# Moving the loads of the attention tables and small weights behind those of the bias tables in an encoder layer on one Trainium2 core

## The chip, the cores and the metric

The kernel runs on one NeuronCore of one Trainium2 chip. The metric is device time in microseconds (us) of one execution; lower is better. The profile is one execution recorded by the hardware profiler. TensorE does the matmuls (PE in the rows, PEld for its weight loads), VectorE is DVE, ScalarE is ACT, GpSimd is POOL, and SyncE (SP, its queue SPq) issues every load and store of this kernel.

## The reference

One layer of a hybrid encoder over 768 tokens (512 of one request, 256 of another) of width 1024. One input projection feeds three groups of heads: A is chunked spatial gating, B differential attention with a distance penalty, C neighbourhood attention on a 64-wide grid with a learned bias. Cut to what matters here:

```python
h = x @ w_in                                   # 768 x 1024 -> u, v (A); q, k, v (B); q, k, v (C)
out_a = gelu(u) * (w_s @ layer_norm(gelu(v), a_ln_g, a_ln_b) + b_s)
lam = exp(sum(lq1 * lk1)) - exp(sum(lq2 * lk2)) + lam_init
out_b = rms_norm((softmax(q1 k1 - slope * dist) - lam * softmax(q2 k2 - slope * dist)) v, subln_g) * (1 - lam_init)
out_c = softmax(q k + bias(rpb)) v             # over a window of rows and 16 columns
x = layer_norm(alpha * x + concat(out_a, out_b, out_c) @ w_out)
x = layer_norm(alpha * x + (silu(x @ w_gate) * (x @ w_up)) @ w_down)
```

## The kernel before, in words

All matmuls run at full fp32 accuracy by splitting: each operand becomes a high part in fp32r (a ScalarE cast, line 113) and a low part (source minus high part, line 114, mostly on VectorE), and three matmuls stand for one product. An operand is thus ready only when a load has landed, ScalarE has cast it and VectorE has subtracted.

**The opening** (lines 262 to 295) computes q and k of branch C. The contraction over 1024 is done in eight steps k of 128. Step k needs tile k of the transposed input, 384 KB (`load_x`, line 230), and every second step a weight tile of 512 KB (`w_load`, line 121). In each step TensorE does 24 matmuls into eight PSUM regions (`cqk_mm`, line 258): for each of four column groups f, first high input with high weights, then low input (`xlo`), then high input with low weights. Inputs and weights share three buffers of the pool `raw`, so a load goes out when the split of an earlier tile has freed one. In what follows w1 is the second weight tile (steps 2 and 3), and x2 and x3 are the inputs of steps 2 and 3.

**After the loop**, in the text of the kernel, come the loads of small tables (lines 298 to 312): `dist` (448 KB, branch B's distances), `lq` (four vectors of 64), `subg` (128 values), `alng` and `alnb` (256 values each), `wsT` (256 KB) and `bsT` (2 KB). The seven vectors are read through `broadcast_rows`, which sends one row of memory to all 128 partitions. Lines 314 to 323 then make `neglam` (two VectorE reductions at 318, a ScalarE Exp at 320, two small VectorE operations) and scale `subg` (line 323).

**Behind them** stand the evacuation of C's q and k from PSUM (`c_evac`, lines 335 to 355), the load of `mask` (line 378, 128 x 1408 fp32, which is 704 KB), and for each of four heads twelve small loads of the relative bias (`rpb`, lines 385 and 390) with seven GpSimd operations that make the bias tables `cb` (lines 394 and 400). Then come the projections of C's v, B, A, with the attention units of C (`c_unit`, line 489) from 7.75 on the kernel's own cost clock and those of B (`b_unit`, line 565) from 61.0 mixed between them, the output projection, and the feed-forward layer (lines 1010 and 1043), which is about two thirds of the time.

What sets the order: TensorE's order is the order of the program text (`manual_schedule`, line 79), with costs and due times written out by hand (lines 34 to 43). The order on every other engine and on SP's queue is set by the framework's scheduler, which simulates the program and gives each engine what is ready, earlier program text first. So a load whose buffer is free from the start may be issued long before the text around it. Within an engine or queue instructions start in the order so chosen; one that waits holds those behind it. In the rows the loads of lines 299 to 312 stand in SP's queue amid the loads of the opening.

`tc.issue_after(ins)` makes the instructions that its block issues on `ins`'s queue stand behind `ins` there, without a wait for its end.

Of the kernel before, what the change touches and what calls it, by code (L numbers as in the profile page):

```python
# [8 lines left out]
F32 = mybir.dt.float32  # L9
F32R = mybir.dt.float32r  # L10
ALU = mybir.AluOpType
AF = mybir.ActivationFunctionType
PSUM = bass.MemoryType.PSUM

P = 128
# [9 lines left out]
LAM0 = 0.8 - 0.6  # L25
# [28 lines left out]
def broadcast_rows(ap, n):  # L54
    return bass.AP(tensor=ap.tensor, offset=ap.offset, ap=[[0, P], [1, n]])
# [3 lines left out]
def encoder_layer(ctx: ExitStack, tc, a, o):  # L59
    nc = tc.nc  # L60
    V, S, G, TE = nc.vector, nc.scalar, nc.gpsimd, nc.tensor
# [179 lines left out]
    attp = att.enter_context(tc.tile_pool(name="att", bufs=1, reuse_waits="tile"))  # L241
# [53 lines left out]
    w_done(3)  # L295


    dist = attp.tile([P, 896], F32, name="dist")
    nc.sync.dma_start(out=dist, in_=a["dist"])
    lq = attp.tile([P, 4, 64], F32, name="lq")  # L300
    for i, n in enumerate(("lq1", "lk1", "lq2", "lk2")):
        nc.sync.dma_start(out=lq[:, i], in_=broadcast_rows(a[n], 64))
    subg = attp.tile([P, P], F32, name="subg")
    nc.sync.dma_start(out=subg, in_=broadcast_rows(a["subg"], P))
    alng = attp.tile([P, 256], F32, name="alng")
    nc.sync.dma_start(out=alng, in_=broadcast_rows(a["alng"], 256))
    alnb = attp.tile([P, 256], F32, name="alnb")
    nc.sync.dma_start(out=alnb, in_=broadcast_rows(a["alnb"], 256))
    wsT = attp.tile([P, 4, P], F32, name="wsT")
    nc.sync.dma_start(out=wsT, in_=a["wsT"])  # L310
    bsT = attp.tile([P, 4], F32, name="bsT")
    nc.sync.dma_start(out=bsT, in_=a["bsT"])

    neglam = attp.tile([P, 1], F32, name="neglam")
    lsum = attp.tile([P, 2], F32, name="lsum")
    lpr = attp.tile([P, 64], F32, name="lpr")
    for i in range(2):
        V.tensor_tensor_reduce(out=lpr, in0=lq[:, 2 * i], in1=lq[:, 2 * i + 1], op0=ALU.mult, op1=ALU.add,
                               scale=1.0, scalar=0.0, accum_out=lsum[:, i:i + 1])
    S.activation(out=lsum, in_=lsum, func=AF.Exp)  # L320
    V.tensor_tensor(out=neglam, in0=lsum[:, 1:2], in1=lsum[:, 0:1], op=ALU.subtract)
    V.tensor_scalar(out=neglam, in0=neglam, scalar1=LAM0, scalar2=None, op0=ALU.subtract)
    V.tensor_scalar(out=subg, in0=subg, scalar1=1.0 - LAM0, scalar2=None, op0=ALU.mult)

    def qk_tiles():
# [51 lines left out]
    for h in range(4):  # L380
        t = mxp.tile([P, 1536], F32, tag="mx", name="cb")
        raw = mxp.tile([P, 1536], F32, tag="mx", name="rpb")
        src = a["rpbs"]
        for r in range(8):
            nc.sync.dma_start(out=raw[16 * r:16 * r + 16, 0:489],
                              in_=bass.AP(tensor=src.tensor, offset=src.offset + h * 945 + r * 63,
                                          ap=[[1, 16], [1, 489]]))
        src = a["rpbp"]
        for r in range(4):
            nc.sync.dma_start(out=raw[32 * r:32 * r + 32, 512:989],  # L390
                              in_=bass.AP(tensor=src.tensor, offset=src.offset + h * 1905 + (4 + r) * 127,
                                          ap=[[1, 32], [1, 477]]))
        for c0, n in ((0, 489), (512, 477)):
            G.tensor_scalar(out=raw[:, c0:c0 + n], in0=raw[:, c0:c0 + n], scalar1=8.0, scalar2=None, op0=ALU.mult)

        def fill(d0, nb, e, row, rows, cols):
            win = raw[:, e:e + 1]
            win = bass.AP(tensor=win.tensor, offset=win.offset, ap=[win.ap[0], [-cols, nb], [-row, rows], [-1, cols]])
            view = [x[:, d0:d0 + nb * P].rearrange("p (b r c) -> p b r c", b=nb, r=rows) for x in (t, mask)]
            G.tensor_tensor(out=view[0], in0=win, in1=view[1], op=ALU.subtract)  # L400


        fill(0, 2, 488 - 16, 63, 8, 16)
        fill(256, 3, 488, 63, 8, 16)
        fill(640, 2, 488, 63, 8, 16)
        for j in range(2):
            fill(896 + 256 * j, 2, 988 - 32 * (1 - j), 127, 4, 32)
        cbias.append(t)


    def proj_nat(w0, evac):
# [821 lines left out]
```

## Time and profile before

| | |
|---|---|
| runs | 893.86 us median of 3 (892.22 to 894.37) |
| the profiled execution's own time | 893.67 us |
| its span | 891.8 us |
| mean granted TensorE clock | 0.995 |
| TensorE busy | 846.5 us, 95% of the span |
| VectorE, ScalarE, GpSimd busy | 75%, 47%, 43% |
| DMA | 66.66 MB, 75 GB/s over the span |

The execution's time is 1.9 us over the span (start and end around the recorded instructions). Busy shares are averages over stages with different limits; what the change touches lies in the first 60 us. A row of a timeline reads: start, duration, engine, line, operation, output and inputs, shape, count, and in brackets the idle time before it with what ended it.

### The profile page before, as it was taken

How to read it: one execution, taken by the hardware profiler on the slowest of the kernel's cores; microseconds unless marked ns; L12 is line 12 of the kernel's file. 1: busy time of each engine (PE TensorE's matmuls, PEld its weight loads, DVE VectorE, ACT ScalarE, POOL GpSimd, SP SyncE). 2: the span in 40 equal slices, each digit the busy share in tenths (PEclk: the TensorE clock that was granted, in tenths of full speed). 3: DMA queues.
4: the chain of work that ended last, by engine and by line, in shares of the span. 5: the costliest groups of instructions: out<-in, count | busy, mean ns of one | idle time of the engine just before them, and what ended most of it. 6: DMA issues, size and time to landing. Idle time of an engine off the chain costs nothing. (4 is left out here: it accounts for less than half of the span.)

```text
span 891.8 us, 12955 instructions
## 1 busy us (share of the span) xinstructions
PE 846.5 (95%) x4811; PEld 754.3 (85%) x4811; DVE 666.9 (75%) x1168; ACT 422.0 (47%) x922; POOL 384.7 (43%) x320
## 2 busy tenths in 40 slices
PE   7999999999999998899999999999999999899996
PEld 6889897888987887898888898898888888789985
DVE  3574447576677568769989897988979797989577
ACT  3375477676665526544434444344444344344421
POOL 0580011100121148877655655555466464653235
PEclk9999999999999999999999999999999999999999
DMA  6830202011017101112212121222121222222222
GB/s 220 247 113 24 71 26 71 24 49 46 5 54 276 54 18 50 46 48 72 72 38 81 48 82 61 72 71 72 70 71 48 71 72 71 71 70 73 72 83 107
DMA packets 22160, 66.66 MB, mean 75 GB/s; under 512 B 3664, under 2 KB 5584, under 8 KB 22096
## 3 DMA queue, kind: packets, MB, share of 16 engines
q1 hardware_dynamic: 22096, 65.82, 22.4%
q8 instruction: 38, 0.62, 0.3%
q14 instruction: 26, 0.21, 0.1%
HBM read 62.67 MB, written 3.15 MB: 74 GB/s over the span
## 5 line engine op out<-in xcount | busy, mean ns | idle before, releaser
L114 DVE TENSOR_TENSOR w<-raw,w 128x512 fp32r<-128x512 f32 (+2 forms) x179 | 185.1, 1053 | 36.3 <-ACT w L113 35.4
L113 ACT CAST w<-raw 128x512 fp32r<-128x512 f32 (+2 forms) x213 | 138.3, 676 | 119.1 <-POOL raw L168 43.8
L1010 PE MATMUL ff<-x,w 128*128 128x384 f32 x600 | 109.9, 336 | 1.7 <-DVE bv L991 1.7
L1010 PEld LDWEIGHTS ff<-x,w 128*128 128x128 f32 x600 | 105.3, 188 | 3.5 <-DVE bv L991 2.0
L1010 PE MATMUL ff<-mix,w 128*128 128x384 f32 x480 | 91.8, 339 | 14.5 <-ACT snap L1021 6.5
L1010 PEld LDWEIGHTS ff<-mix,w 128*128 128x128 f32 x480 | 83.4, 188 | 19.3 <-DVE bv L1026 9.6
L444 PE MATMUL mm<-xhi,w 128*128 128x512 f32 x320 | 79.1, 346 | 0.4 <-DVE qs L341 0.4
L168 POOL TENSOR_TENSOR ws<-raw 128x512 f32<-128x512 f32 x29 | 41.2, 1424 | 79.2 <-DMA raw<-in_w 74.9
L168 POOL TENSOR_TENSOR raw<-raw 128x512 f32<-128x512 f32 x49 | 71.2, 1454 | 6.7 <-DVE w L114 3.5
L423 PE MATMUL mm<-w,xhi 128*128 128x256 f32 x384 | 71.4, 286 | 0.0
L842 PE MATMUL mm<-w,mix 128*128 128x512 f32 x270 | 68.3, 399 | 1.5 <-ACT tt L686 0.8
L1010 PE MATMUL ff<-xt,w 128*128 128x384 f32 x360 | 65.9, 335 | 0.0
L621 POOL TENSOR_TENSOR mn<-mn,neghalf 128x1 f32<-128x1 f32 x24 | 13.8, 574 | 116.6 <-DVE mn L620 112.8
L1010 PEld LDWEIGHTS ff<-xt,w 128*128 128x128 f32 x360 | 63.0, 188 | 0.0
L1043 PE MATMUL ff<-w,mix 128*128 128x512 f32 x216 | 58.2, 400 | 4.9 <-DVE y L1048 4.9
L842 PEld LDWEIGHTS mm<-w,mix 128*128 128x128 f32 x270 | 49.2, 188 | 12.6 <-ACT tt L686 1.3
L423 PEld LDWEIGHTS mm<-w,xhi 128*128 128x128 f32 x384 | 58.1, 189 | 1.4 <-issue 0.9
L444 PEld LDWEIGHTS mm<-xhi,w 128*128 128x128 f32 x320 | 49.1, 189 | 6.8 <-issue 0.8
L114 DVE TENSOR_TENSOR mix<-bv,mix 128x384 fp32r<-128x384 f32 x62 | 52.9, 856 | 2.1 <-ACT mix L113 2.0
L114 POOL TENSOR_TENSOR w<-raw,w 128x512 fp32r<-128x512 f32 x34 | 49.6, 1475 | 10.5 <-ACT w L113 10.2
L1043 PE MATMUL sc<-w,mix 128*128 128x512 f32 x189 | 50.4, 398 | 3.4 <-DVE y L1048 3.4
L423 PE MATMUL mm<-w,xlo 128*128 128x256 f32 x192 | 53.4, 278 | 0.0
(234 smaller groups left out, 1772.8 us busy)
## 6 DMA issues: line engine op xcount, KB each, us to landing
raw<-in_w SPq DMA_DIRECT2D x95, 512.0 KB, 3.3
y<-in_x SPq DMA_DIRECT2D x6, 512.0 KB, 9.2
out_y<-y SPq DMA_DIRECT2D x12, 256.0 KB, 2.0
raw<-in_xT SPq DMA_DIRECT2D x7, 384.0 KB, 5.2
ln<-in_lng SPq DMA_DIRECT2D x2, 512.0 KB, 7.2
ln<-in_lnb SPq DMA_DIRECT2D x2, 512.0 KB, 7.6
rpb<-in_rpbs SPq DMA_DIRECT2D x32, 30.6 KB, 3.4
rpb<-in_rpbp SPq DMA_DIRECT2D x16, 59.6 KB, 3.1
```

Source lines behind the costliest of these rows:

```text
L113: S.copy(out=hi, in_=src)
L114: eng.tensor_tensor(out=lo, in0=src, in1=hi.bitcast(F32), op=ALU.subtract)
L168: G.tensor_tensor(out=out, in0=in0, in1=in1, op=f)
L423: TE.matmul(ps, lhsT=x[:, k, t * P:(t + 1) * P], rhs=w[:, wi, sl], start=(k == 0 and x is xhi and wi == 0), stop=(k == KT - 1 and x is xlo))
L444: TE.matmul(p, lhsT=w[:, wi, sl], rhs=x[:, k, c0:c1], start=(k == 0 and wi == 0 and x is x_hi), stop=(k == KT - 1 and wi == 1))
L621: G.tensor_tensor(out=mn[:, 7:8], in0=mn[:, 7:8], in1=neghalf[:, 0:1], op=ALU.pow)
L842: TE.matmul(ps, lhsT=mix[OUT_ORDER[i]][:, m, t * P:(t + 1) * P], rhs=w[:, wi, sl], start=(i == first and m == 0 and wi == 0), stop=(i == l ...
L1010: TE.matmul(b, lhsT=w[:, wi, k * P:(k + 1) * P], rhs=x1_block(x_name[prod], m, k), start=(prod in (1, 2, 5) and k == 0 and wi == 0 and m = ...
L1043: TE.matmul(b, lhsT=gt_block(a_slot[prod], m)[:, t * P:(t + 1) * P], rhs=w[:, wi], start=(prod in (1, 2, 5) and m == 0 and wi == 0), stop= ...
```

## The change

The loads of lines 299 to 312 and the operations of lines 317 to 323 move, in the text, behind the loop that makes the four bias tables. The loads are put in a block that is to be issued behind the last `rpb` load of the fourth head. Nothing is added or removed: the same ten loads, six VectorE operations and one Exp.

```diff
-    dist = attp.tile([P, 896], F32, name="dist")
-    nc.sync.dma_start(out=dist, in_=a["dist"])
-    lq = attp.tile([P, 4, 64], F32, name="lq")
-    for i, n in enumerate(("lq1", "lk1", "lq2", "lk2")):
-        nc.sync.dma_start(out=lq[:, i], in_=broadcast_rows(a[n], 64))
...
-    S.activation(out=lsum, in_=lsum, func=AF.Exp)
...
-    V.tensor_scalar(out=subg, in0=subg, scalar1=1.0 - LAM0, scalar2=None, op0=ALU.mult)
...
         for r in range(4):
-            nc.sync.dma_start(out=raw[32 * r:32 * r + 32, 512:989],
-                              in_=bass.AP(tensor=src.tensor, offset=src.offset + h * 1905 + (4 + r) * 127,
-                                          ap=[[1, 32], [1, 477]]))
+            rpb_load = nc.sync.dma_start(out=raw[32 * r:32 * r + 32, 512:989],
+                                         in_=bass.AP(tensor=src.tensor, offset=src.offset + h * 1905 + (4 + r) * 127,
+                                                     ap=[[1, 32], [1, 477]])).ins
...
         cbias.append(t)
+
+
+    dist = attp.tile([P, 896], F32, name="dist")
+    lq = attp.tile([P, 4, 64], F32, name="lq")
+    subg = attp.tile([P, P], F32, name="subg")
+    alng = attp.tile([P, 256], F32, name="alng")
+    alnb = attp.tile([P, 256], F32, name="alnb")
+    wsT = attp.tile([P, 4, P], F32, name="wsT")
+    bsT = attp.tile([P, 4], F32, name="bsT")
+
+    with tc.issue_after(rpb_load):
+        nc.sync.dma_start(out=dist, in_=a["dist"])
+        for i, n in enumerate(("lq1", "lk1", "lq2", "lk2")):
+            nc.sync.dma_start(out=lq[:, i], in_=broadcast_rows(a[n], 64))
+        nc.sync.dma_start(out=subg, in_=broadcast_rows(a["subg"], P))
+        nc.sync.dma_start(out=alng, in_=broadcast_rows(a["alng"], 256))
+        nc.sync.dma_start(out=alnb, in_=broadcast_rows(a["alnb"], 256))
+        nc.sync.dma_start(out=wsT, in_=a["wsT"])
+        nc.sync.dma_start(out=bsT, in_=a["bsT"])
+
+    neglam = attp.tile([P, 1], F32, name="neglam")
+    lsum = attp.tile([P, 2], F32, name="lsum")
+    lpr = attp.tile([P, 64], F32, name="lpr")
+    for i in range(2):
+        V.tensor_tensor_reduce(out=lpr, in0=lq[:, 2 * i], in1=lq[:, 2 * i + 1], op0=ALU.mult, op1=ALU.add,
+                               scale=1.0, scalar=0.0, accum_out=lsum[:, i:i + 1])
+    S.activation(out=lsum, in_=lsum, func=AF.Exp)
+    V.tensor_tensor(out=neglam, in0=lsum[:, 1:2], in1=lsum[:, 0:1], op=ALU.subtract)
+    V.tensor_scalar(out=neglam, in0=neglam, scalar1=LAM0, scalar2=None, op0=ALU.subtract)
+    V.tensor_scalar(out=subg, in0=subg, scalar1=1.0 - LAM0, scalar2=None, op0=ALU.mult)
```

## Rows read from the trace of the kernel before

**Rows 1.** The page's first part: busy time, share of the span, instructions.

```profile
PE 846.5 (95%) x4811; PEld 754.3 (85%) x4811; DVE 666.9 (75%) x1168; ACT 422.0 (47%) x922; POOL 384.7 (43%) x320
```

**Rows 2.** Busy time by stage: stretch, length, five engines, granted clock, DMA share, GB/s.

```profile
0.00:45.00 45.00, 39.89 (x200) 33.21 (x200) 19.53 (x28) 16.49 (x24) 13.09 (x16) 0.96 0.73 232
45.00:106.00 61.00, 60.69 (x444) 52.80 (x445) 32.95 (x96) 36.91 (x94) 18.08 (x18) 1.00 0.21 67
...
400.00:860.00 460.00, 437.18 (x2261) 399.42 (x2260) 396.01 (x541) 191.43 (x371) 246.23 (x175) 1.00 0.21 68
```

**Rows 3.** Timeline of TensorE, end of step 1 to the start of step 4.

```profile
15.05 0.28 PE L258 MATMUL av<-xhi,w 128*128 128x256 f32 x1
15.60 0.62 PE L258 MATMUL mm<-xhi,w 128*128 128x512 f32 x2 [0.27 <-ACT xhi L113]
18.33 0.86 PE L258 MATMUL mm<-xlo,w 128*128 128x512 f32 x2 [2.11 <-DVE xlo L114]
...
23.83 0.51 PE L258 MATMUL mm<-xhi,w 128*128 128x512 f32 x2
...
28.02 0.51 PE L258 MATMUL mm<-xhi,w 128*128 128x512 f32 x2
```

**Rows 4.** Busy time by microsecond in the opening, columns as in rows 2.

```profile
5.00:6.00 1.00, 0.35 (x2) 0.00 (x0) 0.00 (x0) 0.32 (x1) 0.00 (x0) 1.00 0.93 269
...
14.00:15.00 1.00, 1.00 (x7) 0.91 (x6) 0.15 (x1) 1.00 (x2) 0.00 (x0) 1.00 0.20 62
...
17.00:18.00 1.00, 0.00 (x0) 0.00 (x0) 0.82 (x2) 0.00 (x0) 0.00 (x0) 1.00 0.45 169
...
20.00:21.00 1.00, 1.00 (x5) 0.85 (x4) 0.46 (x1) 0.00 (x0) 0.00 (x0) 0.50 1.10 432
...
22.00:23.00 1.00, 1.00 (x7) 0.89 (x6) 0.00 (x0) 0.00 (x0) 0.00 (x0) 1.00 0.96 351
```

**Rows 5.** Timeline of VectorE around the low part of step 2's input.

```profile
14.85 1.23 DVE L114 TENSOR_TENSOR w<-raw,w 128x1024 fp32r<-128x1024 f32 x1 [2.58 <-ACT w L113]
...
17.18 0.23 DVE L323 TENSOR_SCALAR subg<-subg 128x128 f32<-128x128 f32 x1 [0.97 <-DMA subg<-in_subg]
17.32 0.95 DVE L114 TENSOR_TENSOR xlo<-raw,xhi 128x768 fp32r<-128x768 f32 x1
```

**Rows 6.** Timeline of SP's queue in the opening: when loads are issued.

```profile
3.99 0.43 SPq L299 DMA_DIRECT2D dist<-in_dist  x1
...
7.15 0.33 SPq L121 DMA_DIRECT2D raw<-in_w  x1
...
9.89 0.43 SPq L304 DMA_DIRECT2D subg<-in_subg  x1
```

**Rows 7.** DMA issues of short stretches (those of rows 6): KB, us from issue to landing.

```profile
dist<-in_dist SPq DMA_DIRECT2D x1, 448.0 KB, 5.8
...
raw<-in_w SPq DMA_DIRECT2D x1, 512.0 KB, 6.6
...
subg<-in_subg SPq DMA_DIRECT2D x1, 64.0 KB, 7.3
```

**Rows 8.** The page's DMA issues, whole span: KB each, median us to landing.

```profile
raw<-in_w SPq DMA_DIRECT2D x95, 512.0 KB, 3.3
...
rpb<-in_rpbs SPq DMA_DIRECT2D x32, 30.6 KB, 3.4
```

**Rows 9.** Users of the tile dist: durations in ns, first and last start in us.

```profile
L584 DVE CUSTOM_DVE_ANT_0 p<-sc,dist x48: 407/684/693, 136.3 to 295.5; 128x512 f32<-128x512 f32 x32, 128x256 f32<-128x256 f32 x16
```

**Rows 10.** Timeline of VectorE at branch C's first unit.

```profile
57.17 0.36 DVE L517 TENSOR_SCALAR p<-p,mn 128x256 f32<-128x256 f32 x1
```

**Rows 11.** Timeline of TensorE at branch C's first unit.

```profile
60.41 0.44 PE L523 MATMUL tp<-ident,p 128*128 128x128 f32 x2
```

**Rows 12.** Timeline of SP's queue from the last bias loads on.

```profile
53.63 1.81 SPq L390 DMA_DIRECT2D rpb<-in_rpbp  x4
56.84 82.89 SPq L121 DMA_DIRECT2D raw<-in_w  x8
```

More of the change, by code (lines that the diff above doesn't have):

```diff
@@ L295, in encoder_layer @@
     w_done(3)
-    dist = attp.tile([P, 896], F32, name="dist")
-    nc.sync.dma_start(out=dist, in_=a["dist"])
-    lq = attp.tile([P, 4, 64], F32, name="lq")
-    for i, n in enumerate(("lq1", "lk1", "lq2", "lk2")):
-        nc.sync.dma_start(out=lq[:, i], in_=broadcast_rows(a[n], 64))
[L303 to L319, printed above, removed]
-    S.activation(out=lsum, in_=lsum, func=AF.Exp)
-    V.tensor_tensor(out=neglam, in0=lsum[:, 1:2], in1=lsum[:, 0:1], op=ALU.subtract)
-    V.tensor_scalar(out=neglam, in0=neglam, scalar1=LAM0, scalar2=None, op0=ALU.subtract)
-    V.tensor_scalar(out=subg, in0=subg, scalar1=1.0 - LAM0, scalar2=None, op0=ALU.mult)
     def qk_tiles():
```

## The prediction

> **What bounds the kernel now.** I read the page's busy times first: TensorE is busy 846.5 us of 891.8, 95% [rows 1], and no other engine comes near. So a change counts if it removes TensorE's idle or slow time, and the question is where that lies. Busy time by stage tells it: in the first 45 us TensorE is busy for 39.89, and its granted clock is 0.96 there; from 45 to 106 us it is busy for 60.69 of 61.00 [rows 2]. The stage right behind the opening is thus bound by TensorE alone, and a microsecond won before 45 us can travel. In the feed-forward stage it idles for 23 of 460 us [rows 2], but there it waits for operands made from its own results, and those waits shift with it.
>
> Next, TensorE's timeline in the opening. One undisturbed step of the contraction takes 28.02 - 23.83 = 4.19 us. Step 2 takes from 15.60 to 23.83, 8.23 us, and 0.27 us of idling stands ahead of it [rows 3]. The excess is 8.23 - 4.19 + 0.27 = 4.31 us, in two parts: 2.38 us of idling (0.27 for the high part of x2, 2.11 for its low part), and some 1.9 us of slow matmuls behind that. For the second part see the granted clock: 1.00 until the idle microsecond 17 to 18, 0.50 (1.2 GHz) at 20 to 21, 1.00 (2.4 GHz) again from 22 on. TensorE also idled for most of 5 to 6 us, and there the clock stayed at 1.00 [rows 4].
>
> Why the low part was late, VectorE's timeline tells. It ended the split of w1 at 16.08. TensorE had started on the high part of x2 at 15.60, so that was there. But the low part starts only at 17.32, because in VectorE's order the scaling of `subg` stands ahead of it and waits for that table's load until 17.18 [rows 3, 5]. The table was issued at 9.89 and landed 7.3 us later [rows 6, 7], and nothing needs it for more than a hundred microseconds: the first reader of `dist` starts at 136.3 [rows 9], and `subg` scales B's outputs, which come later still.
>
> The loads themselves were late too. w1, issued at 7.15, took 6.6 us [rows 6, 7], twice the 3.3 that such a load takes over the whole span [rows 8]. The DMA engines were no bottleneck then: at 14 to 15 us, with x3, `subg` and others outstanding, they were 0.20 busy and moved 62 GB/s, while at 20 to 21 they moved 432 GB/s [rows 4]. What was in flight at the slow time and not at the fast time are the small broadcasts (`lq`, `subg`); I take them for the cause, though only the coincidence is in the rows.
>
> **The change, part by part.**
>
> *Six VectorE operations and the Exp leave the opening.* The wait for `subg` goes with them: the low part can start when w1's split ends, 16.08 instead of 17.32, which is 1.24 us, even if no load lands any sooner. What would be left is an idle time of about 0.9 + 0.27 us, and one of that size left the clock at 1.00 at 5 to 6 us [rows 4]. With the clock kept, this part alone brings 1.24 + 1.9 = 3.1 us; without it, 1.2.
>
> *Ten loads leave SP's queue in the opening, others take their places.* `mask` and the `rpb` loads have free buffers from the start, so the scheduler will pull them to the front as it did `dist`. Where w1 had `dist` and two broadcasts ahead of it, it will have `mask` (704 KB for 448) and two small bias loads. The 256 KB more cost 0.6 us at 432 GB/s and 0.95 at 269 [rows 4]; the two broadcasts saved have no price of their own in the rows. So w1's landing is bounded by the quiet 3.3 us [rows 8], 10.5 us, and by 6.6 + 0.95, 14.7 us. I take 13.0, nearer to the crowded row, since a large load still stands ahead. Then ScalarE and VectorE are done with w1 and x2 about 0.75 us sooner, the low part ends at 17.03 - 0.75 = 16.3 where TensorE, through with the high part 15.33 + 0.62 = 15.95, wants it, and some 0.4 us is left of the 4.31. At 10.5 nothing is left, a gain of 4.3; at 14.7 the low part ends near 18.0, the clock falls again, and the gain is 0.3. For later steps the queue ahead of the next weight tile holds small bias loads in place of broadcasts, `wsT` and `mask`, so I expect no new wait. **The opening: -3.9 us**, bounds -0.3 to -4.3.
>
> *GpSimd's bias tables* start sooner with their loads. Their first reader is C's first unit, behind the opening; TensorE does not wait in that stage [rows 2], so this brings nothing. If GpSimd slowed VectorE's splits meanwhile, those have the room: w1's took 1.23 us in a pair of steps of 8.4.
>
> *The tables arrive between the last bias load and C's first units.* That load was issued at 53.63 to 55.4 [rows 12]; with ten loads fewer ahead, the tables take its places, so SP's queue is no longer than before, and no weight load is pushed back by more than their own time. The operations of lines 318 to 323 now stand in VectorE's order near C's evacuation and first unit, and the Exp in ScalarE's. They work for about a microsecond; what matters is how long they wait at the head. Behind them stand C's first scores. Their slack: the first scaled map is done at 57.53 and is transposed at 60.41 [rows 10, 11], so a hold of up to 2.9 us is free. A wait is bounded by zero and by the crowded 7.3 us of `subg` [rows 7], which would cost 7.3 - 2.9 = 4.4. The nearest row is the quiet one, a small load in this same stage: 3.4 us [rows 8], which costs 3.4 - 2.9 = 0.5. I take **+0.6 us**, a little over, since four broadcasts stand in a row.
>
> A rule speaks against moving loads back. The Trainium skill (DMA: Bandwidth & Descriptors, Rules for kernel authors) advises issuing a DMA early and waiting on its semaphore late. For `dist` the trace leaves 75 us even so [rows 9, 12]; for `lq` and `subg` the wait now comes right behind the issue. By the rows above the sum is -3.3; by the rule, with the whole hold paid, it would be -3.9 + 4.4, no gain, and that is a rival below.
>
> **The sum**: -3.9 + 0.6 = -3.3. The profiled execution took 893.67 us, 0.19 under the median of the runs; 893.67 - 3.3 = **890.4 us**. About 0.3% (2.7 us) is what a measurement of this kernel can tell from no change, so the gain is just outside that.
>
> **The rivals.**
>
> *The mask takes the tables' place.* If bytes and not broadcasts made w1 late, it lands near 14.7, TensorE idles some 2 us again and the clock falls: gain 0.3 to 1.2, given back in part; **893.0 us**. For it: the engines were 0.93 busy at 5 to 6 us. Against it: 0.20 at 14 to 15 [rows 4].
>
> *The wait moves along.* VectorE is held for `lq` and `subg` at C's first unit as long as they took in the opening: +4.4 against -3.9, **894.2 us**. For it: the same broadcasts, the same operations waiting at once. Against it: less traffic there, 0.21 of DMA time from 45 to 106 us [rows 2].
>
> *Slower: the tables stand behind a weight load that waits for its buffer.* From 56.84 on SP issues eight weight loads in 82.89 us [rows 12], one in about 11.8, each held until a split frees a buffer. If the scheduler puts one ahead of `lq` or `subg`, VectorE waits half to all of 11.8 us in C's first units; less the slack of 2.9 and with 1.9 for the clock this is +4.9 to +10.8 against -3.9, **894.7 to 900.6**, middle 897.6. It decides from a hold of about 7.6 us on (2.9 slack, 3.9 gain, 2.7 to be seen, less 1.9 of clock). Against it: the table loads have free buffers and come early in the text, so they should fill SP's places before 56.84.
>
> **How the numbers follow.** The forecast, a freed opening with a small hold: 0.66, of which 0.06 falls short of 2.7 us. The mask: 0.11. The wait moved along: 0.13. The queue held: 0.10. Faster by over 0.3%: 0.60; within 0.3%: 0.06 + 0.11 + 0.13 = 0.30; slower: 0.10. The range runs from the whole 4.3 us with no hold (889.4) less 1 us, the half width of the runs shown, to the rivals at 893.0 and, nearly, 894.2: 888.4 to 893.9. Left out are the held queue and a small part of the moved wait.
>
> **What would show it.** Right: no idle time over 1 us ahead of `xlo` in step 2 and a granted clock of 1.00 through 16 to 22 us; w1 landing in under 6 us; TensorE at C's first transposes about 4 us sooner; no broadcast before the last `rpb` load. The hold would show as VectorE idle ahead of line 318 or 323, released by a DMA, between 48 and 60 us. Wrong: 0.50 in the clock of the opening again; TensorE idle from 45 to 106 us above 1.5 us; or a changed order far from the tables, in the feed-forward stage, which I count at nothing since those waits hang on TensorE's own results.

## The result and the profile after

The changed kernel is **slower**: 897.95 us median of 7 runs (895.76 to 900.91) against 893.86 of the kernel before (892.15 to 895.77), ratio 1.0052 with a 95% interval of 1.0038 to 1.0066, or some 4.1 to 4.6 us. Forecast was 890.4 with a range up to 893.9. The changed kernel's profiled execution has a span of 896.7 us.

Busy time by stage, changed kernel, columns as in [rows 2]:

```profile
0.00:45.00 45.00, 42.35 (x223) 35.71 (x224) 25.55 (x31) 23.83 (x37) 23.77 (x25) 1.00 0.76 234
45.00:106.00 61.00, 55.84 (x398) 48.65 (x398) 24.25 (x86) 26.27 (x75) 7.81 (x9) 0.94 0.21 66
...
400.00:860.00 460.00, 437.37 (x2255) 401.26 (x2254) 393.46 (x536) 192.90 (x372) 246.09 (x175) 0.99 0.22 70
```

The opening is as forecast: TensorE is busy for 42.35 us in place of 39.89 and its clock is 1.00. The stage behind it was full before (60.69 of 61.00) and now has 5.2 us of idling and a clock of 0.94. TensorE's timeline says where:

```profile
15.87 0.62 PE L258 MATMUL mm<-xlo,w 128*128 128x512 f32 x2 [0.50 <-DVE xlo L114]
...
41.05 0.51 PE L446 MATMUL mm<-xhi,w 128*128 128x512 f32 x2
...
57.72 1.11 PE L669 MATMUL tp<-ident,vT 128*128 128x128 f32 x4 [5.16 <-ACT vT L661]
...
63.99 0.44 PE L525 MATMUL tp<-ident,p 128*128 128x128 f32 x2
```

Step 2 idles 0.50 us where it idled 2.11 [rows 3]. The projection of C's v starts at 41.05; in the kernel before it started at 45.31, so 4.26 us are won in these two executions. Then TensorE stands for 5.16 us in front of the transposes of C's v (line 669), waiting for ScalarE's copies. C's first map (its first block of softmax weights, `p`) is transposed at 63.99 where it was 60.41 [rows 11]: 3.58 us late. Between the two points 4.26 + 3.58 = 7.84 us were lost, 5.16 of them idle. The rest is the clock, by microsecond:

```profile
56.00:57.00 1.00, 0.00 (x0) 0.00 (x0) 0.76 (x4) 0.15 (x1) 0.00 (x0) 0.84 0.76 298
57.00:58.00 1.00, 0.28 (x2) 0.28 (x3) 0.85 (x5) 0.97 (x4) 0.00 (x0) 0.50 0.70 249
...
62.00:63.00 1.00, 1.00 (x5) 0.85 (x4) 0.00 (x0) 0.00 (x0) 0.00 (x0) 0.50 0.70 279
...
64.00:65.00 1.00, 1.00 (x9) 0.91 (x8) 0.91 (x3) 0.53 (x2) 0.00 (x0) 1.00 0.00 0
```

From 57 to 63 us the granted clock is 0.50, with TensorE busy all the while from 57.72 on: about 2.7 us. That is what [rows 4] showed in the opening, moved to another place.

What held ScalarE, its timeline and VectorE's tell:

```profile
46.09 0.83 ACT L327 CAST kk<-kk 64x768 fp32r<-64x768 f32 x1
56.85 0.20 ACT L407 ACTIVATE lsum<-lsum 128x2 f32<-128x2 f32 x1 [9.93 <-DVE lsum L405]
57.08 0.86 ACT L661 COPY vT<-mm 128x512 f32<-128x512 f32 x2
```

```profile
51.63 0.23 DVE L405 CUSTOM_DVE_ANT_0 lpr<-lq 128x64 f32<-128x64 f32 x1 [5.67 <-DMA lq<-in_lk]
51.78 0.08 DVE L405 DVE_READ_ACCUMULATOR2_ANT lsum<- 128x1 f32 x1
51.90 0.69 DVE L325 TENSOR_TENSOR kl<-tp,kk 64x512 fp32r<-64x512 f32 x1
55.87 0.23 DVE L410 TENSOR_SCALAR subg<-subg 128x128 f32<-128x128 f32 x1 [3.27 <-DMA subg<-in_subg]
56.13 0.43 DVE L325 TENSOR_TENSOR kl<-av,kk 64x256 fp32r<-64x256 f32 x1
56.59 0.23 DVE L405 CUSTOM_DVE_ANT_0 lpr<-lq 128x64 f32<-128x64 f32 x1
```

VectorE waits 5.67 us for the first pair of vectors and 3.27 for `subg`; only then comes the second reduction, for which the Exp in ScalarE's queue waits, 9.93 us in all, with the copies of C's v (line 661) right behind it. The loads came when the text wanted them, right behind the last bias load, from 45.12 on, but they landed late (SP's queue, then the DMA issues of short stretches, us to landing last):

```profile
45.12 0.42 SPq L392 DMA_DIRECT2D dist<-in_dist  x1
...
47.49 0.43 SPq L395 DMA_DIRECT2D subg<-in_subg  x1
```

```profile
raw<-in_w SPq DMA_DIRECT2D x1, 512.0 KB, 5.7
...
lq<-in_lk SPq DMA_DIRECT2D x1, 32.0 KB, 6.9
...
subg<-in_subg SPq DMA_DIRECT2D x1, 64.0 KB, 8.4
```

The first row is w1, 5.7 us in place of 6.6 [rows 7]. The others are the second lk vector and `subg`: 8.4 us, more than the 7.3 of the crowded opening [rows 7], while the DMA engines were 0.04 to 0.28 busy from 48 to 54 us and 0.53 and 0.79 in the two microseconds after. The first of the five small loads took only 3.6 us; issued some 0.47 us apart, they landed at 49.2, 51.6, 51.7, 53.9 and 55.9.

### The profile page after: what moved, and what is told of

It reads as the page before. It is cut to its first block, busy times and chain, and to the rows that moved or that the text cites. A ratio compares the mean times of both kernels' runs of the same rounds, so it can differ in the third digit from the quotient of the medians.

```text
span 896.7 us, 12949 instructions
## 1 busy us (share of the span) xinstructions
PE 851.2 (95%) x4811; PEld 759.8 (85%) x4811; DVE 666.5 (74%) x1168; ACT 422.0 (47%) x922; POOL 383.8 (43%) x320
## 2 busy tenths in 40 slices
DMA packets 22160, 66.66 MB, mean 74 GB/s; under 512 B 3664, under 2 KB 5584, under 8 KB 22096
## 5 line engine op out<-in xcount | busy, mean ns | idle before, releaser
L1012 PE MATMUL ff<-mix,w 128*128 128x384 f32 x480 | 94.0, 345 | 15.4 <-DVE bv L1028 7.5
L1012 PEld LDWEIGHTS ff<-mix,w 128*128 128x128 f32 x480 | 85.4, 192 | 20.2 <-DVE bv L1028 10.5
L844 PEld LDWEIGHTS mm<-w,mix 128*128 128x128 f32 x270 | 49.2, 188 | 12.6 <-ACT tt L688 1.3
L692 POOL TENSOR_TENSOR tt<-tt,xh 128x256 f32<-128x256 f32 x12 | 10.1, 840 | 103.1 <-ACT tt L689 101.6
```

Source lines behind the costliest of these rows:

```text
L692: G.tensor_tensor(out=u["tt"], in0=u["tt"], in1=u["xh"], op=ALU.mult)
L844: TE.matmul(ps, lhsT=mix[OUT_ORDER[i]][:, m, t * P:(t + 1) * P], rhs=w[:, wi, sl], start=(i == first and m == 0 and wi == 0), stop=(i == l ...
L1012: TE.matmul(b, lhsT=w[:, wi, k * P:(k + 1) * P], rhs=x1_block(x_name[prod], m, k), start=(prod in (1, 2, 5) and k == 0 and wi == 0 and m = ...
```

## The experiments

The theory: the opening's gain is real and travels, and all that was lost is the hold at C's first unit, made by small loads that are slow because 128 partitions read one row. The main rival: the loss comes from weight loads or a changed order elsewhere. Two numbers read from TensorE's timeline sum up each run: when the projection of C's v starts, and how long it is from there to the transpose of C's first map. Each ratio is to runs of the kernel before that were made along with it.

| kernel | C's v starts, us | to C's first map, us | ratio (95% interval) |
|---|---|---|---|
| before | 45.31 | 15.10 | 1 |
| changed | 41.05 | 22.94 | 1.0052 (1.0038 to 1.0066) |
| e1: operations late | 41.75 | 14.94 | 0.9966 (0.9956 to 0.9977) |
| e2: operations late, loads early | 46.71 | 14.94 | 1.0014 (1.0001 to 1.0027) |
| e3: changed, rows laid out | 40.55 | 14.93 | 0.9957 (0.9941 to 0.9973) |
| e5: Exp late | 41.57 | 19.66 | 1.0023 (1.0010 to 1.0036) |
| e6: subg late | 41.20 | 17.89 | 1.0000 (0.9989 to 1.0012) |
| e4: before, rows laid out | 41.63 | 14.94 | 0.9956 (0.9938 to 0.9974) |
| e8: e2, rows laid out | 41.84 | 14.97 | 0.9954 (0.9939 to 0.9968) |
| e7: e1, rows laid out | 41.82 | 14.92 | 0.9966 (0.9954 to 0.9978) |

The two columns in us come from one profiled execution each. In those of e1, e4, e7 and e8 the matmuls of the opening run at half speed until about 10 us, in the others until about 7, as a first group of four shows, here in e4 and in the kernel before (TensorE's timelines):

```profile
7.23 1.48 PE L258 MATMUL mm<-xhi,w 128*128 128x512 f32 x4
```

```profile
7.39 0.87 PE L258 MATMUL mm<-xhi,w 128*128 128x512 f32 x4
```

That makes the start of C's v some 1.5 us later in these four (an estimate: half of the 3 us between). The granted clock is given as 1.00 there in all ten traces, so for these first microseconds that column does not tell the speed.

**e1, the operations late.** The operations (the two reductions, the Exp, the two of `neglam` and the scaling of `subg`: six in all, five of them on VectorE, where the texts put on record count seven and six) go into a function that is called at 40 on the kernel's cost clock, and are queued behind operations of a unit of C there; the loads stay behind the bias tables.

```diff
-    for i in range(2):
-        V.tensor_tensor_reduce(out=lpr, ...
+    def table_ops():
+        with tc.issue_after(last["v"]), tc.issue_after(last["s"]):
+            for i in range(2):
+                V.tensor_tensor_reduce(out=lpr, ...
...
-            S.copy(out=hi, in_=src)
-            V.tensor_tensor(out=lo, in0=src, in1=hi.bitcast(F32), op=ALU.subtract)
+            last["s"] = S.copy(out=hi, in_=src).ins
+            last["v"] = V.tensor_tensor(out=lo, in0=src, in1=hi.bitcast(F32), op=ALU.subtract).ins
...
+    later(40.0, table_ops)
```

> The changed kernel with its seven small operations (two reductions, Exp, neglam, scaling of subg) put behind one of branch C's later units, some 40 us further on; the loads stay behind the bias tables. Theory 1, the hold: all that was lost is the wait of VectorE and ScalarE for the small loads at C's first unit, and the opening's gain is whole. Then TensorE idles under 0.7 us between 45 and 106 us, transposes C's first map near 56.2 us (60.41 before), and the time is 3.5 to 4.5 us under before: 889.4 to 890.4, ratio 0.995 to 0.996. Theory 2, the order elsewhere: the loss comes from weight loads behind the broadcasts or from a changed order further on; then the time stays at before or above it, ratio 1.000 to 1.005.

Measured: 889.98 us median, inside the range of theory 1; the ratio, 0.9966, is just above its 0.995 to 0.996. TensorE does not idle between 45 and 106 us (busy time of that stage):

```profile
45.00:106.00 61.00, 61.00 (x449) 53.10 (x449) 30.47 (x100) 32.08 (x88) 7.42 (x8) 1.00 0.23 74
```

C's first map came at 56.69, 3.7 us sooner than before. Theory 2 falls: with the same loads in the same places and only the waits taken away, the loss is gone and the change becomes a gain, 0.3%. The weight tile queued behind `alng` is as late as in the changed kernel (8.8 us, there 8.9) and costs nothing.

**e2, the operations late and the loads early.** The same edit on the kernel before.

> The kernel before, with its loads where they were, in the opening, and only the seven small operations put behind one of branch C's later units. It parts the opening's gain. If the wait for subg at the head of VectorE's queue was what made the low part of step 2 late: it starts at 16.1 to 16.3 us, TensorE idles about 0.9 us there, the clock stays at 1.00, and the time is about 3.1 us under before, ratio 0.9965. If the small loads' slowness was the larger part: the low part is little earlier, the clock falls to 0.50 again, and 1.2 us or less is won, ratio 0.9987 or more.

Measured: 894.04 us, ratio 1.0014: nothing won. What the first reading expected did happen at step 2, and was lost again at step 4. TensorE's timeline:

```profile
16.89 0.61 PE L258 MATMUL mm<-xlo,w 128*128 128x512 f32 x2 [0.76 <-DVE xlo L114]
...
27.50 0.62 PE L258 MATMUL mm<-xhi,w 128*128 128x512 f32 x2 [2.22 <-ACT xhi L113]
28.49 0.82 PE L258 MATMUL mm<-xlo,w 128*128 128x512 f32 x2 [0.37 <-DVE xlo L114]
```

Step 2 starts its low part 1.44 us sooner and the clock stays up. But step 4 now comes too soon for its own loads: TensorE idles 2.22 + 0.37 us there, and the clock falls to 0.50 from 29 to 32 us. What ends the wait is the cast of step 4's input: SP's queue issued that load at 19.89, having waited 1.1 us for `alnb` to land, and it took 6.7 us. The stall at step 2 had covered that; taken alone, its cause is worth nothing.

**e3, the changed kernel with rows laid out.** The seven vectors lie 128 times in memory, so that each partition reads its own row; order and bytes into the core are the same.

```diff
-        nc.sync.dma_start(out=subg, in_=broadcast_rows(a["subg"], P))
+        nc.sync.dma_start(out=subg, in_=a["subg"])
...
-        "subg": inputs["b_subln_g"], "alng": inputs["a_ln_g"], "alnb": inputs["a_ln_b"],
+        **{k: np.repeat(inputs[n], P, axis=0) for k, n in (
...
+            ("subg", "b_subln_g"), ("alng", "a_ln_g"), ("alnb", "a_ln_b"))},
```

> The changed kernel, with the seven vectors laid out in memory 128 times, so that each partition reads a row of its own; same bytes into the core, same order, same operations. If many reads of one row are what makes the small loads slow: lk2 and subg land in 3.5 to 4.5 us (6.9 and 8.4 in the changed kernel), VectorE is through with them by 52 us, TensorE idles about 0.8 us at the transposes of C's v in place of 5.16, the clock stays at 1.00, and the time is about 3.4 us under before, ratio 0.996. If their place in the queue or their small size makes them slow: they land as late as in the changed kernel, and the time is 4 us over before, ratio 1.0045.

Measured: 889.38 us, ratio 0.9957. The second lk vector and `subg` land in less than the expected 3.5 us (DMA issues of short stretches):

```profile
lq<-in_lk SPq DMA_DIRECT2D x1, 32.0 KB, 2.6
subg<-in_subg SPq DMA_DIRECT2D x1, 64.0 KB, 2.3
```

VectorE's wait falls from 5.67 to 1.32 us and the one for `subg` is gone (VectorE's timeline):

```profile
47.22 0.23 DVE L405 CUSTOM_DVE_ANT_0 lpr<-lq 128x64 f32<-128x64 f32 x1 [1.32 <-DMA lq<-in_lk]
...
48.21 0.55 DVE L410 TENSOR_SCALAR subg<-subg 128x128 f32<-128x128 f32 x1
```

So neither size nor place makes these loads slow: 32 KB took 6.9 us from one row and 2.6 from 128 rows, at the same place in the same order, and both traces hold the same 22160 packets and 66.66 MB. The operations still wait at the head of VectorE's queue, but within its slack.

**e5, the Exp late.** In the changed kernel only the Exp and the two operations of `neglam` are put off, by the edit of e1.

> The changed kernel with only the Exp and the two operations of neglam put 40 us later; the two reductions and the scaling of subg stay, so VectorE is held as long as in the changed kernel. If the stall reaches TensorE through ScalarE's queue (the Exp ahead of the copies of C's v): the transposes of C's v come near 52.6 us without a wait, and TensorE stops only at the scores of the second unit, near 55.3, until VectorE frees a score bank near 58: 2.5 to 3 us idle in place of 5.16, and the time falls 2.5 to 5 us under the changed kernel, 893 to 895.5, ratio 0.999 to 1.002. If VectorE's own hold is what stops TensorE: 5.2 us of idling as before and ratio 1.0045.

Measured: 894.98 us, inside what was expected if the stall came through ScalarE, and ratio 1.0023, just above it (0.999 to 1.002); and TensorE stops at another place than expected. TensorE's timeline:

```profile
53.34 0.63 PE L673 MATMUL tp<-ident,vT 128*128 128x128 f32 x4 [0.29 <-issue]
56.51 0.41 PE L673 MATMUL av<-ident,vT 128*128 128x128 f32 x2 [2.54 <-DVE kl L325]
```

With ScalarE free the first transposes go ahead almost at once ("issue" is time with no wait that the profile shows), and the next ones stop 2.54 us for a PSUM bank: VectorE's evacuation `kl<-av` (the low part of C's k) stands behind the scaling of `subg`. So either queue holds TensorE; the Exp's place made 22.94 - 19.66 = 3.3 us of the 7.84.

**e6, the scaling of subg late.** The same with line 410 alone.

> The changed kernel with only the scaling of subg put 40 us later. It parts VectorE's hold into its two waits. lk2 lands near 53.9 us, the Exp is through near 54.5, the copies of C's v near 55.3: TensorE idles 2.8 us in place of 5.16, the clock falls still, and the time is 2.4 us under the changed kernel, ratio 1.0015 to 1.003. If the wait for subg were the whole hold: TensorE idles under 1 us and the ratio is 0.996; if the wait for lq were: nothing changes, ratio 1.0045.

Measured: ratio 1.0000, between the 1.0015 to 1.003 expected of two waits and the 0.996 expected if `subg` were the whole hold. TensorE idles nearly what was worked out (2.8):

```profile
55.45 0.66 PE L673 MATMUL tp<-ident,vT 128*128 128x128 f32 x4 [2.74 <-ACT vT L665]
```

But the clock stayed at 1.00 in this execution, so 17.89 - 14.94 = 2.95 us were lost, with no share of the clock in it. The two waits are thus worth about 3 us (`lq`) and 5 us (`subg`, with the clock).

**e4 and e8, rows laid out in the kernel before.** e4 leaves loads and operations of the kernel before in the opening; e8 puts the operations off too, as e2 does.

> The kernel before, loads and operations where they were, with the seven vectors laid out in memory 128 times. If the many reads of one row are the whole cause of the slow opening, neither the place of the loads nor of the operations matters once they are gone: the small loads land in 2.5 to 4 us, w1 in under 5.5, the weight and input of step 4 in time, VectorE does not wait for subg, TensorE idles under 1 us from 8 to 45 us with the clock at 1.00, and the time is 3 to 4.5 us under before, ratio 0.995 to 0.997. If the bytes of dist, wsT and mask ahead of the tiles count as much: step 2 or step 4 still stops by 1 us or more, and the ratio is 0.998 or above.

> The kernel before with both: operations 40 us later and the vectors laid out. With the operations late alone, the stop moved from step 2 to step 4 and nothing was won. If that stop was made by the slow reads: it is gone here, TensorE's start on C's v comes near 41 us in place of 45.3, ratio 0.995 to 0.997, the same as with the laid out rows alone. If it was made by the place of the loads: step 4 stops by 2 us as before, ratio near 1.000.

Measured: 890.33 us, ratio 0.9956, and 889.45 us, ratio 0.9954. In neither does TensorE wait once between 8 and 45 us. In e4 VectorE does not stop for `subg`, which was issued early and waited for at the same place as before (VectorE's timeline):

```profile
14.33 0.22 DVE L318 CUSTOM_DVE_ANT_0 lpr<-lq 128x64 f32<-128x64 f32 x1
...
14.48 0.22 DVE L323 TENSOR_SCALAR subg<-subg 128x128 f32<-128x128 f32 x1
14.62 0.95 DVE L114 TENSOR_TENSOR xlo<-raw,xhi 128x768 fp32r<-128x768 f32 x1
```

So the reads of one row account for the opening's 4 us, and with them gone no place of the loads or operations that was tried stops TensorE or differs clearly in time. One expectation was missed: in e4 the small loads still took 4.7 to 5.4 us, not 2.5 to 4 (5.7 to 7.3 in the kernel before), so one row is not all that slows them in the opening; the DMA engines were 0.80 busy over its 45 us, and whether that is the rest was not tried. e8 closes e2: its stop at step 4 was made by those reads, not by the place of the loads. There step 4's weights and input are issued at 14.77 and 15.71, in e2 at 17.94 and 19.89.

**e7, all three.** The loads behind the bias tables, the operations late, the rows laid out.

> The changed kernel with both: operations 40 us later and the vectors laid out. If the two mend the same loss: no better than either alone, ratio 0.995 to 0.997, TensorE idle under 0.3 us from 45 to 106 us. If they mend different parts: 2 us or more better than either, ratio under 0.9935.

Measured: 890.15 us, ratio 0.9966: no better than either alone. The two edits mend one loss.

## Why the prediction was wrong

*The opening, -3.9 us: right, and by its own signs.* 4.26 us were won between two profiled executions; w1 landed in 5.7 us, at 12.6 where the sum took 13.0; 0.50 us of idling was left at step 2 where it took 0.4; the clock stayed up. One premise was weaker than it looked: the 1.00 at 5 to 6 us [rows 4] lies in the stretch where that column does not tell the speed; that a short idle leaves the clock up is shown by e2 (0.34 and 0.76 us at step 2). What I called a coincidence in the rows, that the broadcasts slow the loads around them, e4 showed to be the cause (w1 in 5.3 us, no wait at step 2 or 4).

*One half of it was wrong all the same.* The part that counts VectorE's wait for `subg` as worth 3.1 us "even if no load lands any sooner" fell with e2: nothing is won, since the next loads are late by as much. A stall found by the wait that ends last is worth only what the next wait leaves, and that one is not in the trace of before.

*The step that failed is the hold at C's first units, +0.6 us; it was +7.84.* Its sign came as the text had named it: VectorE idle ahead of both operations between 48 and 60 us, released by a DMA. Three things were mis-sized in it.

The wait. For loads read by 128 partitions from one row I took the 3.4 us of a bias load [rows 8], because that row stood in the quiet stage, and set aside the 7.3 us of `subg` itself [rows 7] as crowded. The same text had argued that these broadcasts are slow on their own account. The first of them took 3.6 us, near that row, but those that VectorE waited for last took 6.9 and 8.4 us with the engines nearly idle for most of it, and 2.6 and 2.3 with the rows laid out (e3): the likeness that counted here was the kind of access, and by the landing times how many stand in a row, not the traffic.

The slack. I read 2.9 us from the first map's scaling to its transpose [rows 10, 11]. But the hold reached TensorE by another way: the Exp stands in ScalarE's queue ahead of the copies of C's v. Before, ScalarE's and TensorE's timelines have

```profile
55.58 0.86 ACT L659 COPY vT<-mm 128x512 f32<-128x512 f32 x2
```

```profile
56.81 0.60 PE L667 MATMUL tp<-ident,vT 128*128 128x128 f32 x4
```

that is, a slack of 56.81 - 56.44 = 0.37 us behind a weight cast that stood ahead of the copies there. The room in the changed order was larger: in e5 the copies end at 51.03 and the transposes start at 53.34, 2.3 us later. Either is less than the 2.9 taken. The moved Exp was named in the prediction, but what stands behind it was not looked for. And VectorE's waits stood ahead of the last evacuations of C's k, which hold a PSUM bank (e5), not only ahead of the scores.

The clock. I charged 1.9 us for it in the opening and in the slower rival, and left it out of the hold; it cost about 2.7 behind 5.16 us of idling.

*The rivals.* "The wait moves along" is what happened. It was priced at 4.4 us by the 7.3 us row less the 2.9 of slack; with a slack of 0.4 and the 1.9 charged for the clock elsewhere it is 7.3 - 0.4 + 1.9 = 8.8, and so slower than before. The one named for slower, a weight load ahead of the tables in SP's queue, did not happen: the load at 48.49 stands behind `subg`. "The mask takes the tables' place" did happen in the queue and cost nothing. The Trainium skill's advice (DMA: Bandwidth & Descriptors, Rules for kernel authors: issue early, wait late) is right here in its second half: e1 differs from the changed kernel by late waits alone and is some 7.7 us faster (0.9966 against 1.0052). Its first half does not hold here for these loads: issued early, with late waits, they win nothing (e2), because they slow others; with the rows laid out early issue costs nothing (e8).

*From the first map to the end* the 3.58 us became 4.9 in the profiled spans and 4.1 between the medians; the stretch from 340 to 400 us had a clock of 0.94 in this execution. Whether that is chance is left open; the kernel before, e1 and e3 have 0.97 there, e8 has 0.94 and e5 0.91.

## What to carry to other kernels

When an operation that waits for a load is moved, list for each engine that takes part what will stand behind it in that queue, and take the smallest slack among all of them; here a 0.2 us Exp carried VectorE's waits into ScalarE's queue, and with it alone put off C's first map came 3.3 us sooner after the start of C's v (e5). Read that slack in the order that the change will make, not only in the old one. Price a wait by a row of the same kind of access before one of the same stage. And of the two ways to mend this kernel, the one that removes the cause (rows laid out, 0.9954 to 0.9957; the copies are made where the inputs are prepared, outside the measured time) needs no new order, while the one that only moves loads needs the waits moved too (0.9966).

## What the runs showed of the hardware that had not been expected

Loads of 32 and 64 KB in which all 128 partitions read one row of memory took 3.6 (the first of them) and then 5.2 to 8.4 us in the changed kernel, and 2.3 to 3.0 us from rows of their own in the same order (e3); and loads queued behind them come late too (in the changed kernel the weight tile issued at 48.49 took 8.9 us, in e3 the same one 4.3). Why one row is slow was not tried.

In these profiled executions, whether the clock falls does not follow from the length of an idle time alone. It fell to 0.50 behind 2.11 us (before, step 2), 2.22 us (e2) and 2.54 us with 0.29 ahead of it (e5), and it stayed at 1.00 behind 2.74 us (e6). By microsecond, e5 and then e6:

```profile
56.00:57.00 1.00, 0.49 (x4) 0.48 (x5) 0.94 (x4) 0.00 (x0) 0.00 (x0) 0.99 0.62 240
57.00:58.00 1.00, 1.00 (x5) 0.90 (x4) 1.00 (x5) 0.87 (x3) 0.00 (x0) 0.50 0.59 212
```

```profile
54.00:55.00 1.00, 0.00 (x0) 0.00 (x0) 0.39 (x3) 0.39 (x2) 0.00 (x0) 1.00 0.58 216
...
56.00:57.00 1.00, 1.00 (x8) 0.91 (x7) 0.35 (x1) 1.00 (x3) 0.00 (x0) 1.00 0.66 260
```

A stall of this size was thus worth its idle time plus either nothing or some 1.9 us (step 2 in the kernel before, and 19.66 - 14.94 less 2.83 of idling in e5), and a forecast should carry both.
